# A decoder kernel on one core: the opening of its projection, with row transposes, sample and memory rows, parameter loads and one copy put at other places

## The chip, the cores and the metric

The kernel runs on one core of a Trainium2 chip. The metric is the device time of one execution in microseconds (us). A core has five engines that run side by side: TensorE (PE) for matmuls and transposes, VectorE (DVE), ScalarE (ACT), GpSimd (POOL), and SyncE (SP), which here only issues DMA transfers. A change is called faster or slower here when the medians differ by more than about 0.3%.

## The reference

One layer of a decoder trunk for a prompt of 2048 tokens and a sample group of 8 sequences with 4 new tokens each. Cut to what matters:

```python
def mixer_layer(x, ...):                       # x: 2048 prompt rows, or 8 x 4 sample rows, of 1024
    h = rms_norm(x, pre_g)
    z = h @ w_in                               # 1024 x 5632, columns in eleven groups of 512
    ca, cb, cg, pu, pg, q, k, v, sg, mq, mg = split(z)
    y_c = conv_branch(ca, cb, ...)             # causal depthwise conv of width 31
    y_p = pool_branch(pu, ...)                 # causal pooling, windows 2/4/8/16
    y_s = sb_fn(q, k, v, sb_bias)              # stick-breaking attention, 8 heads of 64
    y_m = mem_attend(mq, mk, mv)               # 4 heads of 128 into 256 memory tokens
    mix = concat([y_c * silu(cg), y_p * silu(pg), y_s * silu(sg), y_m * silu(mg)])
    return x + rms_norm(mix @ w_out, post_g)

mk, mv = split(rms_norm(mem_prompt, mem_g) @ w_mem_kv)   # 256 memory rows
```

The sample group attends also to 8192 past tokens in a paged cache, has its own conv and pooling history, and its own memory keys and values.

## The kernel before

The work has three long stages: the projection `x @ w_in` with everything that hangs on it, in two parts of 1024 prompt rows (the 32 sample rows ride in the first part); the prompt's attention; and the output projection. While the projection runs, the sample's paged cache is gathered and attended in 64 chunks, paced by the cost of PE's projection work.

Products are made in three matmuls each: every operand is split into a high part (`xhi`, `whi`) and the rest (`xlo`, `wlo`), and high x high, low x high and high x low are added up in PSUM (`mm3`, L237 to L246). A block of 24 such matmuls makes 128 output columns for up to 384 rows. `mm3` yields in the middle of the block.

Before a row can be used it has to be normalised and turned. `norm_rows` (L203) lets ACT take the sum of squares (`row_stats`, L194) and a root (`rstd`, L198), DVE takes the reciprocal and scales the rows (L209). `table` lists the roots in program order; entry 0 is a first root at the start, so that `table[6]` is the root of prompt tile 5. `issue_after(table[-1].ins)` queues each norm behind the one traced before it, on ACT. `split_rows` (L212 to L221) turns half a tile: four transposes on PE into a PSUM tile (three buffers), the copy of the high part on ACT (L219) and the subtraction of the low part on DVE (L220).

The rows come as a generator, `x_first` (from L282): eight prompt tiles of 128 rows (tile 0 to 7) and the 32 sample rows, two yields for each, one behind each half; `X["done", 0]` says how many rows are ready. Behind the second half of a tile it also requests a later tile's load and norms a later tile. Five row buffers (`XB`) are used in turn by these tiles and then by the two memory tiles. Six steps, that is tiles 0 to 2, are done ahead of everything else.

`z_groups` (L800) walks over column groups. The first group has two members, `q0` and `q1`, and the rows come in blocks of 384, 384 and 288 (the last with the sample rows). A block is begun when its rows are done; until then the loop only yields. After each yield the caller lets every live task go one step (`tasks.step`). The memory rows are such a task, `mem_norm` (L385 to L400): it is added when 768 rows are done, requests its loads and norms its two tiles at its first step, waits `MSTEP` yields, and turns half a tile with each further step. The parameters and histories are another, `params_and_histories` (L460 to L499): its first step requests six loads of parameter rows (into one tile, `prow`) and the load of a first history tile; four yields later PE turns the parameters (`pps`), then three history tiles (`hps`), one with each step. Two buffers serve `prow` and the history tiles. In the kernel before it is added when the first column group is through.

A block's result is copied out of PSUM by `z_evac` (from L689), for `q` by ACT with a scale (L697); two PSUM buffers hold blocks.

What sets the order: PE's instructions run in the order of the source (`manual_schedule`). Those of ACT, DVE, POOL and SP are put in order at build time by a planner that keeps dependencies, gives earlier lines of the trace precedence and works with its own estimate of times; each engine then runs its list strictly in that order.

Of the kernel before, what the change touches and what calls it, by code (L numbers as in the profile page):

```python
# [12 lines left out]
AF = mybir.ActivationFunctionType  # L13
# [5 lines left out]
P = 128  # L19
# [38 lines left out]
X0 = 6  # L58
SEND = 0.97
XA = 3  # L60
MSTEP = 4
KT = 2
WR = 2

# [23 lines left out]
def kernel(  # L88
# [9 lines left out]
    pe, act, dve, pool, sp = nc.tensor, nc.scalar, nc.vector, nc.gpsimd, nc.sync  # L98
# [70 lines left out]
    table = [act.activation(out=first, in_=eps_t, func=AF.Sqrt)]  # L169
# [60 lines left out]
    def split_w(raw, nm):  # L230
        lo = wp.tile([P, ND, P], F32R, tag="wlo", name=f"wlo{nm}", bufs=2)
        hi = wp.tile([P, ND, P], F32R, tag="whi", name=f"whi{nm}", bufs=2)
        act.copy(hi, raw)
        (dve if nm in SECOND else pool).tensor_tensor(out=lo, in0=raw, in1=hi.bitcast(F32), op=ALU.subtract)
        return hi, lo
# [15 lines left out]
    tasks = Tasks()  # L251
# [30 lines left out]
    def x_first(tile_):  # L282

        todo = [(xp[P * t : P * (t + 1), :], P, P * t, f"p0_{t}") for t in range(8)] + [(xs, NS, PART, "s")]
        xts = {}

        def load(n):
            if n < len(todo):
                xts[n] = tile_(f"xt{todo[n][3]}")
                sp.dma_start(xts[n][: todo[n][1]], todo[n][0])  # L290

        def norm(n):
            if n < len(todo):
                norm_rows(xts[n], todo[n][1], gpre)

        def split_next():
            it = next(iter(raw))
            with tc.issue_after(table[-1].ins):
                wsplit[it] = split_w(raw.pop(it), "%d%s%d" % it)

        load(0)
        gpre = big("gpre0")[:, :D]
        sp.dma_start(gpre, pre_g[0].partition_broadcast(P))
        load(1)
        next_raw()
        load(2)
        next_raw()
        load(3)
        load(4)
        norm(0)  # L310
        norm(1)
        ahead = 2
        for i, (_, rows, col, nm) in enumerate(todo):
            for hf in range(2):
                split_rows(xts[i], rows, xhi, xlo, col, hf, nm)
                if hf:
                    X["done", 0] = col + rows
                    if i < 2:
                        split_next()
                    load(i + 5)  # L320
                    norm(i + ahead)
                    if i == 2:
                        ahead = 3
                        norm(i + ahead)
                yield
# [59 lines left out]
    def mem_norm(mp, M):  # L385
# [5 lines left out]
        for t in range(2):  # L391
            xt = mp.tile([P, D], F32, tag="xt", name=f"xtm{t}", bufs=XB)
            sp.dma_start(xt, mem_prompt[0, P * t : P * (t + 1), :])
            rows.append(norm_rows(xt, P, mg_bc))
        for _ in range(MSTEP):
            yield
# [292 lines left out]
    def z_evac(part, kind, c, ti, c0, c1, ps, s):  # L689
        a0 = PART * part  # L690
        N = c1 - c0
        np_ = min(c1, PART) - c0
        nm = f"{part}{kind}{c}_{ti}"
        tok = a0 + c0
        if kind in ("q", "k"):
            zt = small(f"zt{nm}")
            act.activation(out=zt[:, :N], in_=ps[:, :N], func=AF.Copy, scale=0.125 if kind == "q" else 1.0)  # L697
            hl = k4(f"hl{nm}", [P, 2, 512], F32R)
            dve.tensor_copy(hl[:, 0, :np_], zt[:, :np_])
            pool.tensor_tensor(out=hl[:, 1, :np_], in0=zt[:, :np_], in1=hl[:, 0, :np_].bitcast(F32),  # L700
                               op=ALU.subtract)
            wq.dma_start((qd if kind == "q" else kd)[c, :, :, tok : tok + np_], hl[:, :, :np_].bitcast(F32))
            if N > np_:
                pool.tensor_copy((qsT if kind == "q" else ksT)[:, c, :], zt[:, np_:N])
            if kind == "k":
                tasks.add(natural(zt, N, np_, tok, c, kp, None, (kso,), nm))
        elif kind == "v":
            zt = small(f"zt{nm}")
            act.copy(zt[:, :N], ps[:, :N])
            tasks.add(natural(zt, N, np_, tok, c, vp, vd, (vso, vsd), nm))  # L710
        elif kind in ("cg", "sg", "pg", "mg"):
            sg = small(f"sg{nm}")
            act.activation(out=sg[:, :N], in_=ps[:, :N], func=AF.Sigmoid)
            if kind == "pg":
                dve.tensor_tensor(out=sg[:, :N], in0=ps[:, :N], in1=sg[:, :N], op=ALU.mult)
                tasks.add(pool_out(c, state["d"], part, c0, c1, ti, sg, s["plw"]))
            elif kind == "mg":
                gt = state["g"][:, c0:c1]
                dve.tensor_tensor(out=gt, in0=ps[:, :N], in1=sg[:, :N], op=ALU.mult)
                if N > np_:  # L720
                    pool.tensor_copy(gms[:, c, :], gt[:, np_:N])
            else:
                dve.tensor_tensor(out=sg[:, :N], in0=ps[:, :N], in1=sg[:, :N], op=ALU.mult)
                gdst = gcd if kind == "cg" else gsd
                wq.dma_start(gdst[c, :, tok : tok + np_], sg[:, :np_])
                if N > np_:
                    if kind == "cg":
                        wq.dma_start(gcd[c, :, SEQ : SEQ + NS], sg[:, np_:N])
                    else:
                        pool.tensor_copy(gss[:, c, :], sg[:, np_:N])  # L730
        elif kind == "ca":
            U = s["U"]
            act.copy(U[:, CH + c0 : CH + c0 + np_], ps[:, :np_])
            if N > np_:
                act.copy(us_s[:, c, :, CH:], ps[:, np_:N].rearrange("p (b t) -> p b t", t=TS))
        elif kind == "cb":
            U = state["U"]
            sg = small(f"sg{nm}")
            act.activation(out=sg[:, :N], in_=ps[:, :N], func=AF.Sigmoid)
            uu = U[:, CH + c0 : CH + c0 + np_]  # L740
            pool.tensor_tensor(out=uu, in0=uu, in1=sg[:, :np_], op=ALU.mult)
            if N > np_:
                uv = us_s[:, c, :, CH:]
                pool.tensor_tensor(out=uv, in0=uv, in1=sg[:, np_:N].rearrange("p (b t) -> p b t", t=TS),
                                   op=ALU.mult)
        elif kind == "pu":
            pf = s["pf"]
            act.copy(pf[:, PH + c0 : PH + c0 + np_], ps[:, :np_])
            if N > np_:
                act.copy(ps_s[:, c, :, PH:], ps[:, np_:N].rearrange("p (b t) -> p b t", t=TS))  # L750
        elif kind == "mq":
            hl = k4(f"mh{nm}", [P, 2, 512], F32R)

            act.activation(out=hl[:, 0, :N], in_=ps[:, :N], func=AF.Copy, scale=-(P ** -0.5))
            dve.scalar_tensor_tensor(out=hl[:, 1, :N], in0=ps[:, :N], scalar=-(P ** -0.5), in1=hl[:, 0, :N].bitcast(F32),
                                     op0=ALU.mult, op1=ALU.subtract)
            if N > np_:
                dve.tensor_copy(mqs[:, c, :], ps[:, np_:N])
            state["att"] += 1
            tasks.add(mem_attend(c, part, c0, np_, hl, state["g"], s["kv"]))  # L760

    def z_close(part, kind, c, s):
# [4 lines left out]
        elif kind == "pu":  # L767
# [4 lines left out]
    GROUPS = {0: [[("q", 0), ("q", 1)]] + [[(k, c)] for k in ("q", "k", "v") for c in range(2 if k == "q" else 0, 4)],  # L772
              1: [[("k", 0), ("k", 1)]] + [[(k, c)] for k in ("k", "v", "q") for c in range(2 if k == "k" else 0, 4)]}
# [1018 lines left out]
    with tc.tile_pool(name="mem", bufs=2, side="right") as mp:  # L1792
        M = {}
        xst = x_first(lambda n: mp.tile([P, D], F32, tag="xt", name=n, bufs=XB))
        for _ in range(X0):
            next(xst)
        tasks.add(xst)
        for _ in z_groups(0, GROUPS[0][:1]):
            tasks.step()
            if X["done", 0] >= XM and not M:  # L1800
                M["gen"] = mem_norm(mp, M)
                tasks.add(M["gen"])
        for _ in M["gen"]:
            pass

        sp.dma_start(conv_sample[0][:, 0 : CH - TS, :], state_conv[0][:, TS:CH, :])
        sp.dma_start(pool_sample[0][:, 0 : PH - TS, :], state_pool[0][:, TS:PH, :])
        sp.dma_start(bias_bc, sb_bias[0].partition_broadcast(P))
        dve.tensor_scalar(out=nbias_bc, in0=bias_bc, scalar1=-1.0, scalar2=None, op0=ALU.mult)
        tasks.add(params_and_histories(mp))  # L1810
        mem = mem_tokens(mp, M)
        for _ in z_groups(0, GROUPS[0][1:4], mem):
            tasks.step()
        for _ in range(3):
            tasks.step()
# [291 lines left out]
```

## Time and profile before

| what | value |
|---|---|
| three runs | 2420.32, 2414.77, 2420.05 us |
| median | 2420.05 us |
| profiled execution | 2411.48 us |
| its span, first to last instruction | 2409.8 us |
| granted TensorE clock, mean | 0.985 |
| DMA traffic | 562.14 MB, mean 233 GB/s |

The profile is one execution of the program, taken by the hardware profiler. A row of its timeline gives start and duration in us, engine, line of the kernel, operation, what is written and read, the shapes, and in brackets how long the engine had been idle before and what ended that wait. PEld is the weight load that runs beside PE. SPq is SP's queue of DMA issues: the time there is that of the issue, not of the transfer. A table by stretch gives the busy time of each engine, the TensorE clock that was granted (1.00 is full) and the share of the DMA engines.

### The profile page before, as it was taken

The page shows a single profiled execution, that of the slowest core. Times are in us where ns is not written, and L with a number is a line of the kernel's source. Part 1 is how long each engine was busy: PE and PEld are TensorE (multiplying, and loading weights), DVE is VectorE, ACT ScalarE, POOL GpSimd, SP SyncE. Part 2 cuts the span into 40 slices and gives each one's busy share as a digit, 9 for nine tenths or more (in the row PEclk, how much of TensorE's full clock was granted, in tenths as well). Part 3 has the DMA queues.
Part 4 walks back from the last instruction along what each step waited for, and adds up shares of the span by engine and source line. Part 5 has one row for each costly group of instructions (what it writes and reads, how often), then busy time and mean ns, then how long its engine had stood idle before and what let it go on. Part 6 is the DMA issues. An engine that isn't in the chain of part 4 may idle for free. (4 is left out here: it accounts for less than half of the span.)

```text
span 2409.8 us, 42118 instructions
## 1 busy us (share of the span) xinstructions
PE 2283.9 (95%) x15962; PEld 1772.1 (74%) x15962; DVE 1733.3 (72%) x2420; ACT 1118.2 (46%) x1939; POOL 1288.0 (53%) x1323
## 2 busy tenths in 40 slices
PE   6999999999999999999999998899999998989896
PEld 6898888898888777777777776455555556768775
DVE  5433685959756754577877878879898846686998
ACT  5332344242442322224242435788989955443554
POOL 2553535556564555546556554667876754453430
PEclk9999999999999999999999999999999999999998
DMA  5688988887778899987877767734333217887764
GB/s 178 199 266 277 342 303 308 302 267 263 258 254 308 288 353 321 320 278 267 277 267 269 261 222 176 242 78 117 88 89 81 64 63 245 269 275 247 252 234 165
DMA packets 340437, 562.14 MB, mean 233 GB/s; under 512 B 28481, under 2 KB 212929, under 8 KB 323834
## 3 DMA queue, kind: packets, MB, share of 16 engines
q1 hardware_dynamic: 284858, 290.72, 38.9%
q0 software_dynamic: 55376, 268.72, 31.5%
q8 instruction: 126, 2.06, 0.3%
q14 instruction: 77, 0.63, 0.1%
HBM read 469.28 MB, written 90.68 MB: 232 GB/s over the span
## 5 line engine op out<-in xcount | busy, mean ns | idle before, releaser
L970 DVE STREAM_TRANSPOSE T<-kt 128x1024 f32<-128x1024 f32 x256 | 308.5, 1226 | 191.9 <-PE sSA L983 180.4
L937 POOL DMA_INDIRECT vt<-in_cache_v_dram,idv x256 | 254.0, 992 | 251.0 <-PE sO L1022 190.1
L626 DVE SCALAR_TENSOR_TENSOR cacc<-U,par,cacc 128x512 f32<-128x512 f32 x480 | 360.2, 750 | 11.5
L1323 POOL TENSOR_TENSOR be<-be,E 128x512 f32<-128x512 f32 (+2 forms) x320 | 303.7, 956 | 116.1 <-DVE E L1314 47.9
L1314 DVE TENSOR_TENSOR_SCAN E<-gam,cr,ZM 128x513 f32<-128x513 f32 x192 | 232.8, 1262 | 14.7 <-ACT gam L1299 14.7
L937 POOL DMA_INDIRECT kt<-in_cache_k_dram,idk x128 | 127.7, 998 | 202.4 <-DVE T L970 164.7
L1334 PEld LDWEIGHTS AT<-ident,be 128*128 128x128 f32 x1088 | 117.3, 142 | 126.3 <-ACT at L1340 45.3
L1927 PE MATMUL acc<-wohi,mh 128*128 128x512 f32 (+1 forms) x480 | 194.1, 404 | 1.8 <-DVE mh L1692 1.1
L1299 ACT ACTIVATE gam<-S,nbias_bc 128x1024 f32<-128x1024 f32 (+1 forms) x160 | 172.6, 1079 | 49.4 <-issue 19.4
L1927 PE MATMUL acc<-wolo,mh 128*128 128x512 f32 (+1 forms) x480 | 190.2, 396 | 0.0
L1927 PE MATMUL acc<-wohi,ml 128*128 128x512 f32 x448 | 178.9, 399 | 11.0 <-DVE ml L1692 11.0
L1294 PE MATMUL S<-kT,Q 128*128 128x512 f32 (+1 forms) x640 | 177.2, 400 | 6.4 <-ACT be L1301 2.6
L1301 ACT ACTIVATE be<-S,bias_bc 128x1024 f32<-128x1024 f32 (+1 forms) x160 | 171.6, 1072 | 0.0
L1334 PE MATMUL AT<-ident,be 128*128 128x128 f32 x1088 | 157.5, 283 | 13.8 <-ACT at L1340 4.2
L1350 PE MATMUL av<-at,V 128*64 128x512 f32 (+3 forms) x640 | 152.5, 554 | 1.7 <-DVE sbo L1355 1.7
L983 PE MATMUL sSA<-T,W 128*32 128x128 f32 x4096 | 140.5, 276 | 4.4 <-DVE T L970 2.5
L983 PEld LDWEIGHTS sSA<-T,W 128*32 128x32 f32 x4096 | 105.0, 109 | 42.7 <-issue 36.0
L1692 DVE TENSOR_TENSOR ml<-mr,mh 128x512 fp32r<-128x512 f32 x108 | 99.9, 930 | 37.6 <-ACT mh L1681 37.4
L1294 PEld LDWEIGHTS S<-kT,Q 128*128 128x128 f32 x640 | 106.7, 195 | 22.6 <-ACT be L1301 3.5
L1022 PE MATMUL sO<-vt,saT 128*32 128x512 f32 x1024 | 122.3, 592 | 0.0
L1311 DVE TENSOR_TENSOR_SCAN E<-gam,ZM 128x128 f32<-128x128 f32 (+3 forms) x128 | 96.5, 802 | 29.9 <-ACT gam L1299 23.6
L1340 ACT COPY at<-AT 128x512 f32<-128x512 f32 x192 | 109.1, 657 | 14.4 <-PE AT L1334 14.4
(573 smaller groups left out, 6034.2 us busy)
## 6 DMA issues: line engine op xcount, KB each, us to landing
Q<-qd SPq DMA_DIRECT2D x64, 256.0 KB
mr<-mixd SPq DMA_DIRECT2D x32, 512.0 KB
mr<-mixd SPq DMA_DIRECT2D x48, 256.0 KB
wor<-in_w_out_dram SPq DMA_DIRECT2D x20, 512.0 KB
xtp<-in_x_prompt_dram SPq DMA_DIRECT2D x16, 512.0 KB
kT<-kd SPq DMA_DIRECT2D x64, 128.0 KB
wor<-in_w_out_dram SPq DMA_DIRECT2D x32, 256.0 KB
msd<-mr SPq DMA_DIRECT2D x32, 256.0 KB
```

What stands on the lines that cost most here:

```text
L626: dve.scalar_tensor_tensor(out=ps, in0=U[:, a + k : a + k + H], scalar=wd[:, k : k + 1], in1=ps, op0=ALU.mult, op1=ALU.add)
L937: pool.indirect_dma_start(out=dst, out_offset=None, in_=rows, in_offset=bass.IndirectOffsetOnAxis(ap=idx, axis=0))
L970: S["turn"] = dve.transpose(T[:, 2 * hh : 2 * hh + 2].rearrange("p s j t -> p (s j t)"), kt[:, 2 * hh : 2 * hh + 2].rearrange("p s j d -> ...
L983: pe.matmul(sSs[n][32 * g : 32 * g + 32, P * ml : P * (ml + 1)], lhsT=W[:, jj, :], rhs=T[:, :, jj, :], start=i == 0, stop=i == 3, tile_pos ...
L1294: pe.matmul(S[:, j, :w], lhsT=Q[hh][:, x, P * (q2 + j) : P * (q2 + j + 1)], rhs=KT[hp, hh, kc][:, :w], start=x == 0, stop=x == 1)
L1299: act.activation(out=ga[:, :, 512 - w : 512], in_=S[:, :, :w], func=AF.Sigmoid, bias=nbias_bc[:, h : h + 1], scale=-1.0)
L1301: act.activation(out=be[:, :, :w], in_=S[:, :, :w], func=AF.Sigmoid, bias=bias_bc[:, h : h + 1])
L1314: dve.tensor_tensor_scan(out=E[:, j][:, ::-1], data0=ga[:, j][:, ::-1], data1=ZM[:, 0:1].to_broadcast([P, 513]), initial=carry[hh, q2][:, ...
L1323: pool.tensor_tensor(out=be[:, j, :m], in0=be[:, j, :m], in1=E[:, j, 513 - w : 513 - w + m], op=ALU.mult)
L1334: pe.transpose(ap_[:, P * qt : P * (qt + 1)], A[hp, qb, kc, hh, qt][:, P * r : P * (r + 1)], ident)
L1350: pe.matmul(av[64 * hh : 64 * hh + 64, c], lhsT=V[:, 4 * kc + r, 64 * hh : 64 * hh + 64], rhs=ats.pop((hp, qb, kc, r, hh))[:, c], start=dg ...
L1927: pe.matmul(o[:rows], lhsT=m[a][:, k, :rows], rhs=W[prod, 4 * h + k][w], start=not cont and h == k == n == 0, stop=h == 1 and k == 3 and n ...
```

## The change

```diff
-MSTEP = 4
+MSTEP = 5
...
     x_first:
         for i, (_, rows, col, nm) in enumerate(todo):
+            if rows < P:
+                yield
+                yield
             for hf in range(2):
                 split_rows(xts[i], rows, xhi, xlo, col, hf, nm)
...
     z_evac:
         if kind in ("q", "k"):
             zt = small(f"zt{nm}")
-            act.activation(out=zt[:, :N], in_=ps[:, :N], func=AF.Copy, scale=0.125 if kind == "q" else 1.0)
+            with tc.issue_after(table[6].ins) if nm == "0q0_0" else ExitStack():
+                act.activation(out=zt[:, :N], in_=ps[:, :N], func=AF.Copy, scale=0.125 if kind == "q" else 1.0)
...
         tasks.add(xst)
-        for _ in z_groups(0, GROUPS[0][:1]):
+        params = params_and_histories(mp)
+        for n, _ in enumerate(z_groups(0, GROUPS[0][:1])):
             tasks.step()
+            if n in (0, 2):
+                tasks.step()
+            if n == 4:
+                next(params)
             if X["done", 0] >= XM and not M:
...
-        tasks.add(params_and_histories(mp))
+        tasks.add(params)
```

At the first and the third yield of the first column group the row generator takes two steps instead of one. The sample rows come two steps later, counted from the tile ahead of them. The memory task waits one more step before its first transposes. The first step of the parameter task, its seven load requests, is made in the first column group, at the fifth yield; the rest of it is added as a task at the old place. ACT's copy of the very first block is queued behind the root of tile 5.

## The prediction

> **What bounds the kernel now.** I read the page's first part, then the table of busy time by stretch, to see whether time saved at the front can reach the end.
>
> ```profile
> span 2409.8 us, 42118 instructions
> ...
> PE 2283.9 (95%) x15962; PEld 1772.1 (74%) x15962; DVE 1733.3 (72%) x2420; ACT 1118.2 (46%) x1939; POOL 1288.0 (53%) x1323
> ```
>
> ```profile
> 43.00:52.00 9.00, 3.21 (x19) 2.55 (x17) 6.28 (x10) 6.22 (x15) 0.99 (x1) 0.64 0.00 1
> ...
> 61.00:110.00 49.00, 45.18 (x318) 43.96 (x316) 22.05 (x33) 14.69 (x25) 25.53 (x19) 0.97 0.62 188
> ...
> 200.00:300.00 100.00, 98.99 (x897) 88.22 (x895) 47.97 (x56) 29.49 (x64) 51.00 (x48) 1.00 0.93 324
> ```
>
> The columns are the stretch, its length, then PE, PEld, DVE, ACT and POOL (busy us, count), the granted TensorE clock and the DMA share. TensorE (PE) is busy 95% of the span. Once the projection runs (200 to 300) it is full, at full clock, and its work is issued in one fixed order. So what PE loses in the first 110 us is not made up later, and what it saves there should arrive at the end almost whole. In 43 to 52 PE works 3.21 of 9.00 us at a clock of 0.64; in 61 to 110 it lacks 3.8 us. Who it waits for there, from the list of PE's waits over the first 170 us (total, times, longest):
>
> ```profile
> PE xpss L217 <- DVE xts L209: 3.6, 1, 3.6
> PE pps L485 <- DMA prow<-in_pool_scale_dram: 2.9, 1, 2.9
> PE xpsm L217 <- DVE xtm L209: 2.2, 1, 2.2
> ...
> PE z0q L243 <- ACT xhi L219: 1.5, 1, 1.5
> ...
> PE hps L494 <- DMA ht<-in_state_conv_dram: 0.9, 1, 0.9
> ```
>
> These five are 11.1 us. The change touches the work on both sides of every one, and slow matmuls follow some of them, which this view does not count.
>
> **The order that the change writes.** PE's order is the order of the source; ACT, DVE, POOL and SP are put in order by a planner at build time. Write q0a, q0b for the two halves of a block of 24 matmuls; 3a, 3b for the transposes of the halves of prompt tile 3; S for the sample rows, M0 and M1 for the memory rows. Counting yields:
>
> before: q0a 3a q0b 3b q1a 4a q1b 4b 5a 5b | q0a 6a q0b 6b q1a 7a q1b 7b Sa M0a Sb M0b | q0a M1a q0b M1b ...
>
> after: q0a 3a 3b q0b 4a q1a 4b 5a q1b 5b | q0a 6a q0b 6b q1a 7a q1b 7b M0a Sa M0b Sb M1a | q0a M1b q0b ...
>
> A bar is a new column block. No matmul and no transpose is added or removed; only places move. Four edits follow from it.
>
> **Edit 1, rows 3 to 5 earlier.** Now three sets of transposes stand directly ahead of the second block:
>
> ```profile
> 29.32 1.47 PE L217 MATMUL xpsp<-ident,xtp 128*128 128x128 f32 x12
> 32.24 0.44 PE L243 MATMUL z0q<-xhi,whi0q 128*128 128x384 f32 x1 [1.45 <-ACT xhi L219]
> ...
> 34.99 0.60 PE L217 MATMUL xpsp<-ident,xtp 128*128 128x128 f32 x4
> 35.35 0.42 PE L243 MATMUL z0q<-xhi,whi0q 128*128 128x384 f32 x1
> ```
>
> ```profile
> 23.58 1.28 DVE L209 SCALAR_TENSOR_TENSOR xtp<-xtp,rs,gpre 128x1024 f32<-128x1024 f32 x1
> ...
> 34.02 0.68 DVE L220 TENSOR_TENSOR xlo<-xpsp,xhi 128x512 fp32r<-128x512 f32 x1
> ```
>
> A set of four costs 35.35 - 34.99 = 0.36 us, and the half that begins at 35.35 follows at that pace: 12 matmuls take (from 32.24) about 2.2 us warm. Without a wait the block would start at 29.32 + 3 x 0.36 = 30.40, and 6a would follow at 32.57 instead of 34.99: 2.42 us. The wait is for ACT's copy of tile 5's first half, transposed a moment before. The block's first half does not need the second half: the DVE row at 34.02 is that half's low part, and it lands after matmuls of the block have begun. After, 5a stands a whole q1b (about 2.2 us) ahead of the block and 5b is needed only by q0b, 2.5 us later; the copy and subtraction take about 2 us after a set begins (34.99 to the low part). **Saved: 2.4 us.** What 5a reads is there in time: tile 5 was scaled by 24.86 (the row at 23.58), and 5a now stands at about 27.4.
>
> **Edit 2, sample and memory rows.**
>
> ```profile
> 42.59 0.60 PE L217 MATMUL xpsp<-ident,xtp 128*128 128x128 f32 x4
> 46.82 0.60 PE L217 MATMUL xpss<-ident,xts 32*128 32x32 f32 x4 [3.63 <-DVE xts L209]
> ...
> 50.61 0.63 PE L217 MATMUL xpss<-ident,xts 32*128 32x32 f32 x4
> 51.17 1.11 PE L217 MATMUL xpsm<-ident,xtm 128*128 128x128 f32 x4
> 51.94 0.59 PE L243 MATMUL z0q<-xhi,whi0q 128*128 128x288 f32 x1
> ...
> 54.96 0.98 PE L217 MATMUL xpsm<-ident,xtm 128*128 128x128 f32 x4
> 55.67 0.41 PE L243 MATMUL z0q<-xhi,whi0q 128*128 128x288 f32 x1
> ```
>
> The first half of block three starts 9.35 us after 7b, where the five sets ahead of it would cost 5 x 0.36 = 1.8. It then runs cold: 51.94 to 54.96 is 3.02 us, where the warm pace scaled by columns, 2.2 x 288/384, is 1.63; and M1a behind it costs 0.71 for 0.36. Together 7.55 + 1.4 + 0.35 = 9.3 us are lost here, the most that this edit can bring back. The cause is not the order on PE but ACT, which comes to the sample rows last:
>
> ```profile
> 43.71 1.05 ACT L196 ACTIVATE sq<-xts 32x1024 bf16<-32x1024 f32 x1
> ...
> 46.04 0.18 ACT L196 ACTIVATION_READ_ACCUMULATOR sq<-xtm 128x1 f32 x1
> 47.46 0.27 ACT L219 CAST xhi<-xpss 128x128 fp32r<-128x128 f32 x1 [1.24 <-PE xpss L217]
> 47.62 0.30 ACT L199 ACTIVATE rs<-rs,eps_t 128x1 f32<-128x1 f32 x1
> 47.82 1.04 ACT L196 ACTIVATE sq<-xtm 128x1024 bf16<-128x1024 f32 x1
> ```
>
> ```profile
> 49.84 2.05 DVE L209 SCALAR_TENSOR_TENSOR xtm<-xtm,rs,mg_bc 128x1024 f32<-128x1024 f32 x1
> ```
>
> ACT takes the squares of the sample rows at 43.71, behind its copy for 7b, with its input long loaded (below). The second root, of M0, waits from 46.22 (46.04 + 0.18) to 47.62 behind the copy of the sample's transposes, which PE had to make first. After, M0a stands ahead of Sa on PE, so no plan can put M0's root behind the sample's copy: 1.4 us off M1's chain, whose scaling now ends at 51.89 and then at about 50.5. But block three now has M1a ahead of it: PE has M0a from about 48.1, and five cold sets, three like 51.17 to 51.94 (0.77) and two like 50.61 to 51.17 (0.56), bring it to 51.5. That is 0.4 us sooner, and M1a (0.71) no longer follows: **saved 1.2 us**, if the planner leaves ACT's order of the three squares where it is relative to 7b. This order is not in the trace of before, so both ends: if the three are planned ahead of 7b's copy the whole 9.3 come back; if M1's squares are planned behind ACT's copies of M0a, Sa and M0b, PE waits for M1a by M1's chain (47.82 to 51.89, 4.1 us) from about 50.7: 54.8 plus a cold set is 55.5, 3.6 us later than 51.94, less the 0.71: 2.9 us lost. I take 1.2, the row-by-row case.
>
> **Edit 3, early parameter loads.** pps waits for the last of six small loads:
>
> ```profile
> 75.49 0.41 PE L485 MATMUL pps<-ident,prow 36*128 36x36 f32 x4 [2.94 <-DMA prow<-in_pool_scale_dram]
> 75.83 0.39 PE L243 MATMUL mz<-mhi,whi0mem 128*128 128x256 f32 x1
> ...
> 80.28 0.58 PE L494 MATMUL hps<-ident,ht 120*128 120x120 f32 x4
> ...
> 85.92 0.37 PE L243 MATMUL mz<-mhi,whi0mem 128*128 128x256 f32 x1
> ...
> 88.76 0.34 PE L243 MATMUL z0q<-xhi,whi0q 128*128 128x384 f32 x1
> ```
>
> The wait is 2.94 us. Behind it the clock falls: the 24 matmuls of the memory block from 75.83 end at 80.28 (4.45 us), the same 24 from 85.92 end at 88.76 (2.84 us): 1.6 us more. With the loads out some 30 us sooner both go. The wait of hps (0.9) is for a load that needs the parameters' buffer; pps now comes one step sooner, so that load starts sooner; but the next weights, loaded and split in a chain of their own, then come close, and I count half: 0.5. **Saved: 2.9 + 1.6 + 0.5 = 5.0 us.** The issues cost SP:
>
> ```profile
> 26.45 0.64 SPq L702 DMA_DIRECT2D qd<-hl0q  x1
> 27.18 0.55 SPq L290 DMA_DIRECT2D xts<-in_x_sample_dram  x1
> ...
> 32.13 1.12 SPq L393 DMA_DIRECT2D xtm<-in_mem_prompt_dram  x2
> ...
> 66.81 0.55 SPq L462 DMA_DIRECT2D prow<-in_conv_w_dw_dram  x1
> ...
> 69.04 0.34 SPq L478 DMA_DIRECT2D ht<-in_state_conv_dram  x1
> ```
>
> Seven issues, 66.81 to 69.04 and 0.34 more: 2.6 us of SP. They now join a queue with xts and xtm. If they stand ahead of xtm, xtm is issued at about 35 instead of 32; ACT reads it only after 42, so that cover is some 7 us and the cost nothing; with the cover gone it is at most 2.6 us, inside the lower end of edit 2. In the other direction, xts is now requested ahead of the store at 26.45 that holds it, and its buffer is free after 3b: about 4.5 us sooner, which can only help.
>
> **Edit 4, first copy behind the sixth root.** The sixth root is already done when the copy runs now, and PE's second buffer lets q1 go on. Nothing; were ACT to hold the copy one whole squares instruction (1.05 us, 43.71), q0's next block is still over 5 us away.
>
> **Sum:** 2.4 + 1.2 + 5.0 = 8.6 us. The profiled execution took 2411.48 us (span 2409.8, 1.7 around it), so 2402.9 by its own clock. It lies 8.6 us under the median of the three runs (2414.77 to 2420.32), so such an offset is as large as the effect. Against the median: **2411.4 us**.
>
> [...]
>
> **Rivals.** *The gap closes.* ACT gets the three squares ahead of 7b; for it speaks the sooner request of xts, against it that xtm is not requested sooner. 2.4 + 9.3 + 5.0 = 16.7: 2403.3 us. *The gap widens.* M1's squares land behind copies that wait for PE, as the root at 47.62 does now; 2.4 - 2.9 + 2.9 (the wait of pps without its dip) = 2.4: 2417.6 us. *The dip at 76 is chance*, and comes at another wait all the same: without the 1.6 the sum is 7.0: 2413.0 us. *Slower:* the planner orders ACT, DVE and POOL anew from the moved start on, and in the gather stretch, where PE has no slack, DVE's turns come late:
>
> ```profile
> PE sSA L983 <- DVE T L970: 2.5, 3, 1.4
> ```
>
> Three such waits of 0.83 us stand there today. The stretch has 64 chunks; new waits in a third of them are 21 x 0.83 = 17.5 us: 2420.05 - 8.6 + 17.5 = 2428.9 us. It decides from 11 such waits on (none gained), and 20 make it slower by over 0.3%. Against it speaks that only dozens of instructions at the very front move and the pacing by PE's work is untouched.
>
> **How the numbers follow.** About 0.3%, 7.3 us, is what a measurement here can tell from no change. Chances: forecast 0.38, gap closes 0.25, gap widens 0.18, dip by chance 0.06, slower 0.13. Faster: all of the second, three quarters of the first, half of the fourth: 0.56. Slower 0.14, same 0.30. The range runs from the closed gap less 3 us, half the spread of the three runs, (2400) to the widened one plus the same (2421). The fifth case lies outside, and with it most of what the range leaves out.
>
> **What would show it.** Right: block two follows 5b without a wait; pps and the memory block behind it run at full clock; M0a ahead of Sa; block three starts some 10 us after 7b or sooner. Wrong: ACT's M1 squares behind a copy that waits for PE; new waits of sSA for T; xts still issued behind the store; the wait of pps replaced by one of the memory matmuls for their weights' low part. The largest error would be in edit 2, whose ends lie 12 us apart.

## The result, and the profile after

| | kernel before | changed kernel |
|---|---|---|
| runs on the same chip | 6 | 6 |
| median, us | 2415.65 | 2403.10 |
| lowest to highest, us | 2411.09 to 2420.32 | 2400.27 to 2409.20 |
| ratio of times, 95% interval | | 0.9956 [0.9941, 0.9972] |
| profiled execution (span), us | 2411.48 (2409.8) | 2409.20 (2407.5) |
| granted clock, mean | 0.985 | 0.984 |

The change makes the kernel faster by 0.44%, 10.6 us by the ratio and 12.6 by the medians. Forecast were 8.6, and 2411.4 us; the median of 2403.10 is 8.3 us under that, of which 4.4 are the kernel before, whose median of six runs is 2415.65. The changed kernel's profiled execution is the slowest of its six, so its whole span says little; what follows reads the front of the trace, where a second execution of the changed kernel (changed_again, below) has the two landmarks within 0.01 us.

The table of busy time by stretch, the first two of the three stretches that were shown of before:

```profile
43.00:52.00 9.00, 9.00 (x68) 8.50 (x67) 4.86 (x7) 4.38 (x8) 2.89 (x2) 1.00 0.13 46
61.00:110.00 49.00, 43.17 (x295) 41.27 (x294) 17.13 (x31) 14.24 (x24) 25.03 (x16) 0.93 0.59 185
```

From 43 to 52, PE now works all 9.00 us (3.21 before) at full clock (0.64 before). From 61 to 110 it lacks 5.8 us where it lacked 3.8, and the clock is lower. So the change won more than forecast in one place and lost some in the other. The waits of PE over the first 170 us, without those for the first prompt rows:

```profile
PE nt0k L371 <- ACT zt0k L701: 2.8, 3, 1.3
PE mz L243 <- POOL wlo0mem L234: 2.4, 1, 2.4
...
PE mz L243 <- ACT whi0mem L233: 1.2, 1, 1.2
PE hps L497 <- DMA ht<-in_state_conv_dram: 0.9, 1, 0.9
```

Of the five waits of before only hps is left. Two of mz, a block of memory tokens, for its weights are new: 2.4 + 1.2 us. Those of nt0k come behind 120 us and were 2.0 us before.

To put a price on each stretch I use two landmarks on ACT which every kernel here has: its copy `zt0q` of the block behind the third one, and its first weight split for the next column group, `whi0k`. First before, then the changed kernel:

```profile
65.48 0.49 ACT L697 ACTIVATE zt0q<-z0q 128x384 f32<-128x384 f32 x1 [3.05 <-PE z0q L243]
...
106.78 1.05 ACT L233 CAST whi0k<-wr0k 128x1024 fp32r<-128x1024 f32 x1 [0.58 <-PE z0q L243]
```

```profile
55.57 0.49 ACT L701 ACTIVATE zt0q<-z0q 128x384 f32<-128x384 f32 x1 [3.31 <-PE z0q L243]
...
98.98 1.05 ACT L233 CAST whi0k<-wr0k 128x1024 fp32r<-128x1024 f32 x1 [0.59 <-PE z0q L243]
```

The first landmark comes 65.48 - 55.57 = 9.9 us sooner, the second 106.78 - 98.98 = 7.8. Up to the first landmark lie edits 1 and 2, forecast at 2.4 + 1.2 = 3.6; between the two lies what edit 3 was to save, forecast at 5.0. **The sum of 8.6 against 7.8 is close, but its terms are not: 9.9 instead of 3.6, and 2.1 lost instead of 5.0 saved.** The two errors, 6.3 and 7.1 us, nearly cancel, and that is luck. How the first came about stands on PE around block three:

```profile
32.92 0.60 PE L217 MATMUL xpsp<-ident,xtp 128*128 128x128 f32 x4
...
40.56 0.60 PE L217 MATMUL xpsp<-ident,xtp 128*128 128x128 f32 x4
40.99 0.60 PE L217 MATMUL xpsm<-ident,xtm 128*128 128x128 f32 x4
...
42.56 0.66 PE L217 MATMUL xpsm<-ident,xtm 128*128 128x128 f32 x4 [0.60 <-DVE xlo L220]
...
43.93 0.38 PE L243 MATMUL z0q<-xhi,whi0q 128*128 128x288 f32 x1
...
45.61 0.60 PE L217 MATMUL xpsm<-ident,xtm 128*128 128x128 f32 x4
```

Block three begins 43.93 - 40.56 = 3.4 us behind 7b (9.35 before), and its first half takes 45.61 - 43.93 = 1.68 us (3.02 before). The rows were ready, because ACT took their squares twelve microseconds sooner than before, where they stood at 43.71, at 45.09 (the first row here) and at 47.82. The other rows are of the changed kernel:

```profile
45.09 1.04 ACT L196 ACTIVATE sq<-xtm 128x1024 bf16<-128x1024 f32 x1
```

```profile
30.97 1.04 ACT L196 ACTIVATE sq<-xts 32x1024 bf16<-32x1024 f32 x1
...
32.95 1.06 ACT L196 ACTIVATE sq<-xtm 128x1024 bf16<-128x1024 f32 x1 [0.19 <-DMA xtm<-in_mem_prompt_dram]
...
35.66 1.06 ACT L196 ACTIVATE sq<-xtm 128x1024 bf16<-128x1024 f32 x1 [0.89 <-DMA xtm<-in_mem_prompt_dram]
...
41.19 0.58 ACT L219 CAST xhi<-xpsp 128x512 fp32r<-128x512 f32 x1
```

The second and third are done ahead of the copies of 7a and 7b (the last row); ACT even waits for the rows to arrive. That is the rival that I called "the gap closes". And on SP, first one row of before, then the changed kernel:

```profile
18.45 0.84 SPq L1806 DMA_DIRECT2D out_dram<-in_state_conv_dram  x1
```

```profile
22.94 0.34 SPq L290 DMA_DIRECT2D xts<-in_x_sample_dram  x1
23.32 0.32 SPq L465 DMA_DIRECT2D prow<-in_conv_w_dw_dram  x1
...
28.77 0.55 SPq L396 DMA_DIRECT2D xtm<-in_mem_prompt_dram  x1
...
31.01 0.35 SPq L396 DMA_DIRECT2D xtm<-in_mem_prompt_dram  x1
...
33.67 0.33 SPq L481 DMA_DIRECT2D ht<-in_state_conv_dram  x1
34.04 0.81 SPq L1815 DMA_DIRECT2D out_dram<-in_state_conv_dram  x1
```

The last line has moved: before, SP issued that copy, the store of the sample's conv history from DRAM to DRAM (416 KB), at 18.45, ahead of both `xts` and `xtm`. With the seven small loads in the queue it comes behind them. The memory rows themselves are requested a little sooner (28.77 and 31.01; both from 32.13 on before).

The loss in the second stretch, on PE and on ACT:

```profile
64.73 0.39 PE L243 MATMUL mz<-mhi,whi0mem 128*128 128x256 f32 x1 [1.16 <-ACT whi0mem L233]
...
67.59 0.58 PE L243 MATMUL mz<-mhi,wlo0mem 128*128 128x256 f32 x1 [2.36 <-POOL wlo0mem L234]
...
72.24 0.41 PE L243 MATMUL mz<-mhi,wlo0mem 128*128 128x256 f32 x1
```

```profile
63.26 0.49 ACT L701 ACTIVATE zt0q<-z0q 128x384 f32<-128x384 f32 x1 [4.21 <-PE z0q L243]
63.65 1.04 ACT L233 CAST whi0mem<-wr0mem 128x1024 fp32r<-128x1024 f32 x1
```

ACT's split of the memory weights (`whi0mem`, 63.65) stands behind its copy at 63.26, and that one waits 4.21 us for PE's block. PE, done with it and with a set of transposes, then waits 1.16 us for the split and 2.36 more for the low part that POOL makes of it. Behind the second wait the matmul takes 0.58 us for 0.39, and the table of stretches over that place has the clock at half for six microseconds:

```profile
60.00:64.00 4.00, 3.58 (x24) 3.02 (x22) 1.12 (x4) 0.74 (x2) 0.92 (x1) 1.00 0.35 122
...
67.00:70.00 3.00, 2.40 (x11) 2.41 (x12) 0.00 (x0) 0.00 (x0) 0.54 (x1) 0.50 0.33 91
70.00:73.00 3.00, 2.65 (x13) 2.36 (x12) 0.00 (x0) 0.48 (x1) 0.00 (x0) 0.50 0.98 330
73.00:76.00 3.00, 2.46 (x21) 2.48 (x22) 1.69 (x1) 1.25 (x3) 2.36 (x1) 0.96 0.48 179
```

### The profile page after: what moved, and what is told of

It is laid out like the page before. It is cut to its first block, busy times and chain, and to the rows that moved or that the text cites. A ratio compares the mean times of both kernels' runs of the same rounds, so it can differ in the third digit from the quotient of the medians.

```text
span 2407.5 us, 42122 instructions
## 1 busy us (share of the span) xinstructions
PE 2285.4 (95%) x15962; PEld 1772.8 (74%) x15962; DVE 1728.3 (72%) x2420; ACT 1116.7 (46%) x1939; POOL 1291.0 (54%) x1323
```

## The experiments

Each kernel was run beside the kernel before on one chip, in five rounds, so that a ratio is known to 0.13 to 0.23%. The kernel before has medians of 2407.9, 2408.2 and 2411.6 us in the three groups below, so only ratios and landmarks are compared. The landmarks are those above, as us sooner than in the trace of before; "gap" runs from 7b's transposes to block three.

| kernel | median, us | ratio, 95% interval | gap | 1st landmark | 2nd landmark |
|---|---|---|---|---|---|
| before | | 1 | 9.35 | 0 | 0 |
| changed, first profile | 2403.10 | 0.9956 [0.9941, 0.9972] | 3.4 | 9.9 | 7.8 |
| changed_again | 2397.74 | 0.9959 [0.9946, 0.9973] | 3.4 | 9.9 | 7.8 |
| steps_only | 2400.15 | 0.9969 [0.9955, 0.9982] | 6.1 | 5.7 | 8.6 |
| params_only | 2395.12 | 0.9947 [0.9932, 0.9962] | 2.8 | 8.2 | 11.3 |
| late_params | 2397.96 | 0.9958 [0.9944, 0.9973] | 8.8 | 4.8 | 9.8 |
| split_first | 2393.31 | 0.9931 [0.9908, 0.9953] | 3.4 | 10.7 | 11.6 |
| copies_behind | 2398.44 | 0.9962 [0.9947, 0.9976] | 2.8 | 7.7 | 8.4 |
| steps_copies_behind | 2394.45 | 0.9938 [0.9924, 0.9953] | 3.4 | 11.1 | 11.6 |
| no_row_delay | 2397.88 | 0.9967 [0.9951, 0.9982] | 2.8 | 11.0 | 9.0 |
| histories_ahead | 2392.08 | 0.9921 [0.9907, 0.9934] | 3.4 | 9.9 | 14.7 |
| split_histories | 2396.93 | 0.9937 [0.9923, 0.9950] | 3.4 | 10.8 | 12.4 |

The first group takes the change apart. **My theory** was that edit 3 closes the gap, by what it displaces in SP's queue and so in the planner's order. **The rival** was that edit 2's order on PE closes it, and that edit 3 saves the wait of pps as I had forecast.

**steps_only**: the kernel before with the two double steps alone (edit 1).

```diff
+        for n, _ in enumerate(z_groups(0, GROUPS[0][:1])):
             tasks.step()
+            if n in (0, 2):
+                tasks.step()
```

> The kernel before with only the two double steps of the row generator (edit 1). My theory: the wait in front of the second block goes (2.4 us), and of the gap in front of the third block only a part comes back, because ACT takes the squares of the memory rows only after its copies for 7b and for the sample rows: third block about 6 us after 7b instead of 9.35, parameter stall of 2.9 us still there; in all 4 to 6 us under the kernel before. Rival: the sooner request of the sample rows alone closes the gap: third block within 3.5 us of 7b, 10 us or more under the kernel before.

Part of the gap stays, 6.1 us, and PE waits in it for M0's rows:

```profile
45.06 0.63 PE L217 MATMUL xpsm<-ident,xtm 128*128 128x128 f32 x4 [3.46 <-DVE xtm L209]
...
46.72 0.59 PE L243 MATMUL z0q<-xhi,whi0q 128*128 128x288 f32 x1
```

The wait of pps, though, is gone without edit 3, against what I expected: 0.31 us are left of 2.94. So that wait does not hang on requesting the parameters in the first column group; a planner that starts from other places set their loads otherwise.

**params_only**: the kernel before with edit 3 alone; the requests are made at the seventh yield, which stands at the same place among the row steps.

```diff
+        params = params_and_histories(mp)
+        for n, _ in enumerate(z_groups(0, GROUPS[0][:1])):
             tasks.step()
+            if n == 6:
+                next(params)
...
-        tasks.add(params_and_histories(mp))
+        tasks.add(params)
```

> The kernel before with only the early parameter loads (edit 3), made at the same place of PE's order. My theory: these seven small loads take the place of the long copy of the convolution history in SP's list, the planner then counts on the memory rows sooner, and the squares of sample and memory rows stand ahead of 6b's and 7a's copies on ACT: the gap in front of the third block closes (third block within 3.5 us of 7b) although no row was moved; the wait in front of the second block stays (1.5 us), and a new wait of the second memory block for its weights (3 us or more) takes the place of the parameter stall; in all 6 to 9 us under the kernel before. Rival, as the prediction had it: the gap stays at 9 us and the whole gain is the parameter stall, 5 us.

The gap closes to 2.8 us with no row moved, and block two keeps its wait, since edit 1 isn't there:

```profile
32.26 0.44 PE L243 MATMUL z0q<-xhi,whi0q 128*128 128x384 f32 x1 [1.45 <-ACT xhi L219]
...
45.50 0.38 PE L243 MATMUL z0q<-xhi,whi0q 128*128 128x288 f32 x1
```

The gain, 12.8 us, is larger than I expected: the new wait for the memory weights doesn't come in this kernel.

**late_params**: the changed kernel without edit 3.

```diff
-        params = params_and_histories(mp)
...
-            if n == 4:
-                next(params)
...
-        tasks.add(params)
+        tasks.add(params_and_histories(mp))
```

> The changed kernel without the early parameter loads (edits 1, 2 and 4). My theory: the wait in front of the second block is gone, but the gap in front of the third is 6 us or more, now with M1a behind M1's scaling, and the parameter stall of about 3 us is back; in all 2 to 5 us under the kernel before, and 6 to 9 us above the changed kernel. Rival: moving the rows is what closes the gap; then third block within 4 us of 7b, and only 3 to 5 us above the changed kernel.

The gap is back, 8.8 us, and ACT takes M0's squares late, directly behind its copy for 7b:

```profile
40.47 1.06 ACT L196 ACTIVATE sq<-xtm 128x1024 bf16<-128x1024 f32 x1
```

Edits 1, 2 and 4 do not close it. But both of my times were wrong: pps does not wait here either, the second stretch is 5.0 us shorter than before, and the whole is as fast as the changed kernel. So the open gap costs 5.1 us of the first stretch (4.8 against 9.9; counted from 7b, 6.3), and edit 3 closes it but loses 7.1 in the second (36.3 us against 43.4).

**split_first**: the changed kernel, with ACT's copy held behind the weight split that it had overtaken.

```diff
-        act.copy(hi, raw)
+        hic[nm] = act.copy(hi, raw)
...
+            with (... tc.issue_after(hic["0mem1"].ins) if nm == "0q2_1" else ExitStack()):
                 act.activation(out=zt[:, :N], in_=ps[:, :N], func=AF.Copy, ...)
```

> The changed kernel, with ACT's copy of the second block of q2 queued behind the split of the second memory weight. My theory: the two waits of the second memory block (1.2 and 2.4 us) and the slow clock behind them are only the planner's order on ACT, and the weight has landed in time: they go, and the profile is 4 to 5 us shorter than that of the changed kernel up to 100 us, 13 to 16 us under the kernel before. Rival: the weight's load is late itself; then the same wait stands there for its DMA and nothing is gained.

Both waits of mz go, and the second landmark comes 3.8 us sooner than in the changed kernel (11.6 against 7.8). Counted from landmark to landmark, the second stretch is 3.0 us shorter (95.22 - 54.83 = 40.4 against 98.98 - 55.57 = 43.4). That is less than the two waits with the slow matmuls behind them, 5.6 us (worked out below), since hps, later on, now waits 2.69 us where it waited 0.88, and runs slow itself:

```profile
68.28 1.03 PE L497 MATMUL hps<-ident,ht 120*128 120x120 f32 x4 [2.69 <-DMA ht<-in_state_conv_dram]
```

**changed_again**: the changed kernel once more, beside the second group.

> The changed kernel once more, on the chip on which the other kernels of this call run. If the 5 us by which its first profile fell behind between 60 and 170 us belong to the program (the memory block's wait for its weights) and the later loss of 3 us after 1650 us to that one execution, this profile shows the waits of 1.2 and 2.4 us again, and the later loss not; its median is 10 to 13 us under the kernel before. If the waits too are of one execution, they are not there this time.

Ratio, landmarks and both waits come out as in the first profile. That execution gave back some 5 us behind the second landmark (its span is only 2.3 us under that of before). This one did not: its 2395.55 us are 12.7 under the median of the kernel before in the same group.

The second group asks *what* in edit 3 closes the gap. If the displaced history copy does it, moving that copy alone must do the same.

**copies_behind**: the kernel before with its two history copies issued behind the request of the memory rows, and nothing else.

```diff
-            sp.dma_start(xt, mem_prompt[0, P * t : P * (t + 1), :])
+            M["ld"] = sp.dma_start(xt, mem_prompt[0, P * t : P * (t + 1), :])
...
+        with tc.issue_after(M["ld"].ins):
             sp.dma_start(conv_sample[0][:, 0 : CH - TS, :], state_conv[0][:, TS:CH, :])
             sp.dma_start(pool_sample[0][:, 0 : PH - TS, :], state_pool[0][:, TS:PH, :])
```

> The kernel before with one edit of another kind: the two copies of the sample's old histories from memory to memory are queued behind the loads of the memory rows on SP. No row, no step and no parameter load is moved by hand. My theory (the long copy in front of the memory loads is what made the planner count on them late, and the early parameter loads helped by taking its place): the gap in front of the third block closes as in params_only, third block within 3.5 us of 7b, the wait of 1.5 us in front of the second block stays, and 8 to 13 us are gained. Rival: the copy's place has nothing to do with it, and it was the parameter task's step itself; then the gap stays at 9 us and no more than 3 us are gained.

```profile
19.50 0.33 SPq L462 DMA_DIRECT2D prow<-in_conv_w_dw_dram  x1
...
27.00 0.26 SPq L464 DMA_DIRECT2D prow<-in_conv_b_pw_dram  x1
29.00 0.36 SPq L393 DMA_DIRECT2D xtm<-in_mem_prompt_dram  x1
...
31.18 0.56 SPq L393 DMA_DIRECT2D xtm<-in_mem_prompt_dram  x1
31.80 0.82 SPq L1807 DMA_DIRECT2D out_dram<-in_state_conv_dram  x1
```

```profile
31.60 1.05 ACT L196 ACTIVATE sq<-xts 32x1024 bf16<-32x1024 f32 x1
...
32.98 1.04 ACT L196 ACTIVATE sq<-xtm 128x1024 bf16<-128x1024 f32 x1
...
37.35 1.06 ACT L196 ACTIVATE sq<-xtm 128x1024 bf16<-128x1024 f32 x1 [0.80 <-DMA xtm<-in_mem_prompt_dram]
```

It does: the copy goes to 31.80, the squares of all three come ahead of 7a's and 7b's copies, the gap is 2.8 us. Holding the two stores back saves 9.2 us by the ratio (5.8 to 12.8 by its interval). Over all twelve profiles the rule holds without exception: where the copy is issued ahead of `xtm` (before 18.45, steps_only 23.43, late_params 22.15), ACT has M0's squares at 40.4 or later; where it is issued behind (31.8 to 34.0), at 34 or sooner.

But more than the stores moved. The first two rows show that the planner filled their place with parameter loads, five of the six, of its own accord; before, the first of them came at 66.81. So over the twelve profiles early parameter loads go with the closed gap just as the late copy does, and the first memory load goes with both (issued at 27.9 to 30.0 us where the gap is closed, 32.0 to 33.3 where it is open). Holding the stores back is enough to close the gap, and so is requesting the parameters early; no run here has one without the other.

**steps_copies_behind**: late_params with the copies held in the same way, so edits 1, 2 and 4 without edit 3.

> The changed kernel without the early parameter loads, but with the two history copies queued behind the loads of the memory rows on SP. If both causes are as I think, neither the wait in front of the second block nor the gap in front of the third stands (third block within 3.5 us of 7b), the second memory block does not wait for its weights for more than 1 us, and the kernel is the fastest so far: 14 to 19 us under the kernel before. Rival: closing both brings the next stretch to the weights anyway, as in the changed kernel; then it is 10 to 13 us under the kernel before.

The gap is 3.4 us again without the parameter task's early step, and the second landmark comes 11.6 us sooner. Here too the planner itself issues the first four parameter loads early, at 22.62 to 28.50 us. The second stretch is 40.8 us, 2.6 under the changed kernel's. The gain by the ratio, 15.0 us, is the one expected, but 0.9938 cannot be told from split_first's 0.9931, so it is not shown to be the fastest. What is left in the second stretch is hps, which waits 3.40 us for a history.

**no_row_delay**: the changed kernel without edit 2 (the two yields ahead of the sample rows, and `MSTEP` 5).

> The changed kernel without the two added yields of the sample rows and with the memory rows four steps apart, as before (edit 2 undone). My theory: with the squares planned early the place of the row transposes hardly matters; third block within 3.5 us of 7b, the same waits for the weights, within 2 us of the changed kernel. Rival: the moved rows carry part of the gain; then the third block starts 2 us later or more, and the kernel is 3 us or more slower than the changed one.

Nothing is lost at the front: the gap is 2.8 us, both landmarks come about 1.1 us sooner, no more than the openings of two profiles differ (below), and the second stretch is the changed kernel's to 0.1 us. The ratios, 0.9967 and 0.9959, cannot be told apart. So edit 2 is worth nothing that shows here.

The third group follows the waits to the best version. Both kernels have a third buffer for the parameters and histories and request the second history with the first.

```diff
-        prow = mp.tile([P, 512], F32, tag="ht", name="prow")
+        prow = mp.tile([P, 512], F32, tag="ht", name="prow", bufs=3)
...
+        load()
```

**histories_ahead** adds this to steps_copies_behind.

> steps_copies_behind with a third buffer for parameter and history rows, so that the second history tile is requested with the first. Its profile lost 3.4 us to the wait of hps for that load. My theory: the wait goes (under 0.5 us) and the kernel is 3 to 4 us under steps_copies_behind, 15 to 20 us under the kernel before. Rival: the load lands no sooner in a busy queue, or another wait of the same stretch takes its place; then no gain beyond 1 us.

**split_histories** adds it to split_first.

> split_first with the same third buffer and the second history tile requested with the first. split_first lost 2.7 us to the wait of hps and 4.5 us to three waits of nt0k. My theory: the wait of hps goes (under 0.5 us), and 2 to 4 us are gained on split_first; that the second memory block does not wait for its weights stays so. Rival: what hps no longer waits for, the next weights or nt0k wait for; then no gain beyond 1 us.

```profile
71.13 0.60 PE L498 MATMUL hps<-ident,ht 120*128 120x120 f32 x4 [0.94 <-DMA ht<-in_state_pool_dram]
```

```profile
70.07 0.60 PE L498 MATMUL hps<-ident,ht 120*128 120x120 f32 x4 [2.66 <-DMA ht<-in_state_pool_dram]
```

The wait of hps for the second history goes in both and passes to the next, `in_state_pool`. In histories_ahead that one is short, and the second stretch is 4.2 us shorter than in steps_copies_behind (36.6 against 40.8). This kernel has the lowest ratio of the study: 0.9921 [0.9907, 0.9934], an interval that lies clear of the changed kernel's, though not of those of split_first and steps_copies_behind. In split_histories it is 2.66 us long, the rival's case, and 0.9937 cannot be told from split_first.

## Why the prediction came out right, step by step

**The total** was right: 8.6 us forecast, 10.6 [6.8, 14.3] by the ratio and its interval. The way there was half wrong, and the sum came close by luck, since edits 1 and 2 brought 6.3 us more than forecast up to the first landmark and edit 3 7.1 less behind it. The landmarks account for 7.8 us; whether the rest of the 10.6 is more than the interval was not followed.

**Edit 1** held in mechanism and about in size. Block two follows 5b without a wait, and 6a starts at 32.92 for 34.99: 2.1 us of the 2.4. The two kernels that lack this edit, params_only and copies_behind, keep the wait of 1.45 us.

**Edit 2** is the step that failed, at the words "if the planner leaves ACT's order of the three squares where it is relative to 7b". It did not. The gap went from 9.35 to 3.37 us (6.0), the slow half of block three from 3.02 to 1.68 (1.3), and the set of transposes behind it (M1a before, M1b now) from 0.71 to 0.35 (0.4): 7.7 of the 9.3 that I had named as the upper end, in place of 1.2. I had given this case 0.25; its sum of 16.7 us did not come, because edit 3 lost where it was to save. The cause of the closed gap was filed under the wrong edit as well: no_row_delay, without edit 2, has the closed gap, and late_params, with it, has it open.

**Edit 3** failed in its account of the queue. "If they stand ahead of xtm [...] the cost nothing": I counted the seven loads only as a delay for what stands behind them, and did not ask what else they push back. They pushed back the history copy, and the gap closed. `xtm` was not issued later, at about 35, as I had reckoned for that case, but sooner, at 28.77. That holding back the two stores is enough is shown by copies_behind; that the copy's place alone decides is not, since parameter loads moved up with it. Why the planner then sets ACT's squares early is only argued: where ACT asks early, it has the memory rows at 32.95 and 35.66 us in the changed kernel and the later ones at 37.35 in copies_behind, and in the kernel before it takes them at 45.09 and 47.82 without having waited for them, so it looks as if the planner reckoned the rows behind a large copy to be late and put ACT's squares accordingly.

The 5.0 us of edit 3 itself are another matter. The wait of pps did go, but it goes in steps_only and late_params as well, where the planner set the second stretch up differently without the parameter task's early step. In its place came the two waits for the memory weights that I had named under "what would show it". They cost 1.16 + 2.36 us, and 22 slow matmuls behind them (67.59 to 72.4: 0.212 us each, against 2.84 / 24 = 0.118 in before's fast block) 2.1 more: 5.6 us in place of the 2.94 + 1.6 saved. Split_first shows that the place of one copy on ACT makes these waits.

**Edit 4** is worth nothing, as forecast: with it and without it, the planner writes the same lists of instructions for ACT, DVE, POOL and SP. It was not timed by itself.

**The slow clock behind a wait.** The 1.6 us that I had put behind the 2.94 us of pps stand in the trace of before as 3.42 us at half clock:

```profile
76.22:79.64 3.42, 3.42 (x18) 3.42 (x18) 0.29 (x2) 0.00 (x0) 1.00 (x1) 0.50 0.99 311
```

The runs bear this out, though not as the fixed price that I had made of it. In all twelve profiles I took every wait of PE from 1.8 us up, behind 18 us, that began at full clock, and looked whether the granted clock fell to 0.6 or less within 5 us behind it. After 1.8 to 2.2 us it did so in 19 of 32 cases, after 2.2 to 2.6 us in 15 of 18, after 2.6 to 3.1 us in 20 of 22, above that in 43 of 43. One wait of 1.98 or 1.99 us, late in the kernel, is in every profile, and a dip follows in 8 of the 12. Here it is in params_only and in split_histories, each with the stretch behind it:

```profile
1629.69 1.11 PE L1125 MATMUL nyn<-nanT,vsn 32*64 32x32 f32 x16 [1.99 <-DVE at L1338]
```

```profile
1630.00:1632.00 2.00, 2.00 (x20) 1.51 (x20) 2.00 (x3) 0.36 (x1) 0.63 (x2) 1.00 0.00 0
```

```profile
1634.65 1.91 PE L1131 MATMUL nyn<-nanT,vsn 32*64 32x32 f32 x16 [1.99 <-DVE at L1344]
```

```profile
1634.60:1636.60 2.00, 1.95 (x17) 1.89 (x17) 2.00 (x3) 0.00 (x1) 0.63 (x2) 0.50 0.00 0
```

The same instruction after the same wait runs at 1.00 in the one and at 0.50 in the other. What decides between the two was not shown. In the changed kernel the clock falls at 66.42, behind the 1.16 us of mz and within its next wait of 2.36 us, which ends at 67.59:

```profile
64.73:66.42 1.69, 0.50 (x2) 0.30 (x2) 0.00 (x1) 0.00 (x0) 1.69 (x2) 1.00 0.00 0
66.42:73.25 6.83, 5.06 (x22) 4.77 (x22) 0.00 (x0) 0.73 (x1) 1.12 (x1) 0.50 0.61 199
```

By the counts the 1.6 us behind pps's 2.94 us go with a wait of that length in about nine cases of ten (20 of the 22 above), and the rival that put them down to chance is wrong most of the time.

**The slower rival**, new waits of DVE's turns in the gather stretch, did not come: no kernel here is slower than before.

## What to carry to other kernels

When a planner orders the engines, an edit is not only what it issues but what it displaces: look through each queue for the large transfer that the new work pushes back, and try holding that transfer back by itself, for here two stores held back, the larger by 13 us, were worth 9.2 us, nearly as much as the whole change. Then look what the planner put in their place, or the cause is not yet singled out. Price a front stretch by landmarks that every variant has, stretch by stretch, because a right total can hide two wrong terms. And before filing a saved wait as a gain, look for the next instruction on that path that stands behind a copy waiting for the bottleneck engine.

## What the runs showed of the hardware

Behind 97 of the 115 waits of PE counted above, from 1.8 us up, the granted clock fell to 0.6 or less within 5 us. In the traces of before and of the changed kernel a stretch at 0.50 lasts 3.41 to 10.24 us, the one at the very end of each apart, and they lie at other places: up to 800 us before has one from 45.50 and one from 76.22, the changed kernel one from 66.42 and one from 144.93. Whether single executions of one kernel differ for that reason as they do, 2400.27 to 2409.20 us for the changed kernel on one chip, was not shown.

The opening is not steady. Block one starts at 17.28 us in the profile of the changed kernel and at 17.45 in that of copies_behind, at half pace: soon one matmul every 0.32 us, where it is one every 0.17 or 0.18 from 22.92 on in the one and from 19.51 on in the other. The column of the granted clock reads 1.00 in the changed kernel from 17 us on, but the trace's record of that clock has its first entry only at 22.05 us, so ahead of it the 1.00 says nothing. In the stretch from 20 to 23 us a busy PE gets through 16 instructions in the profiles of before and after, but 21 in that of copies_behind: the moment at which the pace doubles differs, and with it the first landmark, by some 1 us (block two starts at 32.24 in before and at 31.29 in copies_behind, each behind a wait of 1.45 us). Differences between the landmarks of that size are therefore not read here.

The load of one history tile took 6.0 us from its issue to the transposes that waited for it. SP and PE in steps_copies_behind:

```profile
64.16 0.57 SPq L481 DMA_DIRECT2D ht<-in_state_conv_dram  x1
```

```profile
70.18 0.75 PE L497 MATMUL hps<-ident,ht 120*128 120x120 f32 x4 [3.40 <-DMA ht<-in_state_conv_dram]
```

PE saw 3.40 us of it as a wait. In histories_ahead, with a third buffer and this load requested with the first, PE did not wait for it (hps at 65.80 and 67.81).
